# First layer's down-projection: context's product in scaled fp16 parts with four weight blocks in flight, and each late conditioning sum behind an operand's remainder

## The chip, the cores and the metric

One Trainium2 chip, one of its cores. A core has a matrix engine (TensorE: PE in the profile, with PEld for its weight loads), a vector engine (VectorE, DVE), a scalar engine (ScalarE, ACT), GpSimd (POOL) and SyncE (SP); each runs its own list of instructions in order and waits on semaphores for the others. Transfers are issued by queues: SP's carries the loads here, POOL's the stores and a few loads. The metric is the device time of one execution in microseconds, the median of several runs.

## The reference, cut to what matters

Two layers of a diffusion backbone over 1024 latent tokens and 256 context tokens of width 1024. Each layer ends with a gated feed-forward block, whose down-projection `(silu(u @ w_gate) * (u @ w_up)) @ w_down` has an inner width of 2816 (22 blocks of 128). It acts on the latent tokens in both layers and on the context tokens in the first. The residual sum is gated by a conditioning vector: six vectors per layer come from `silu(c) @ ada_w + ada_b`, and six more from the context's own vector with the same weights.

```python
h_lat = h_lat + g2 * swiglu(modulate(rms_norm(h_lat, norm2_g[i]), sh2, sc2),
                            ffn_w_gate[i], ffn_w_up[i], ffn_w_down[i])
if not last:
    h_ctx = h_ctx + cg2 * swiglu(modulate(rms_norm(h_ctx, norm2_g[i]), csh2, csc2),
                                 ffn_w_gate[i], ffn_w_up[i], ffn_w_down[i])
```

All is in fp32, to an accuracy that one pass of a short type doesn't give. The kernel therefore writes an operand as a high part in a shorter type and a remainder, and makes three matmuls for one: high by high, high by remainder, remainder by high.

## The kernel before, in words

The feed-forward of a layer is `ffn`. Its eleven iterations (`i`, two of the 22 blocks each) make the gated hidden values of the latent tokens in a seven-product scheme (Winograd's form of Strassen's), store them as operands of the down-projection, and make the sums of weight quarters that this scheme needs (`sums`: four loads of `down`, vector sums, stores). On the way `bound` takes largest absolute values of what goes into the down-projection, an ACT pass with an accumulator each (L1956); a reduction on DVE and one over the partitions on POOL turn them into scales (`ds`), which bring the operands into fp16's range. Context's hidden values are made before the iterations and stored to `hidc`, 256 KB for two blocks.

`down` follows. Its first part is seven products, p0 to p6. Each is eleven steps, and a step has two operands of 512 columns. `operands` loads both (two loads of 256 KB on SP), ACT makes the high parts in fp16 (L2248, one instruction for each operand) and DVE the remainders (L2249, likewise); twelve matmuls of 128x512 follow (L2258), four groups of columns by three. The last step of a product has its parts in fp32r, not fp16. Two sets of accumulators take turns, and a product's results leave by four DVE instructions at its end (`evict`, L2280).

In the first layer, the late conditioning sums run in between. `ada_stream` has 56 blocks of conditioning weights. The first 30 are done in `ffn`; of the last 26, one is taken at every second step of p0 to p4, and two in p5 (`next(todo)`). Such a block is a load of 512 KB by POOL into one of three tiles of its own and two sums on DVE, each over two instructions of 128x512 and accumulator readings (`step`, whose passes are L571).

After p6, in the first layer alone, comes context's product: 22 weight blocks (`kb`, the loop that ends at L2384). For each, the hidden values are loaded by POOL (128x256) and a weight block of 512 KB by SP, into one of four `ws` tiles or, for every fifth block (`kb % 5 == 4`: 4, 9, 14 and 19), into a tile of the pool S4. ACT casts the high part to fp32r (L352), DVE takes the remainder (L354), and 24 matmuls of 128x256 follow (L2381), eight groups by three. The parts of the weights lie in `pair1()`: one tile tag for the high parts and one for the remainders, two tiles deep. So two blocks are in flight. Beside this product run the normalizations of the results for the next layer (`norm_block`, L673 to L676), which `hook()` strings in.

What sets the order: a scheduler orders every engine's list from the order in the program and its own estimates of time. `with self.follow(x):` has what is inside issued after instruction x. In `ada_stream` only the load of a late block stands in such a bracket (behind the last load by POOL), its sums do not.

Of the kernel before, what the change touches and what calls it, by code (L numbers as in the profile page):

```python
# [10 lines left out]
F32 = mybir.dt.float32  # L11
F32R = mybir.dt.float32r
F16 = mybir.dt.float16
# [245 lines left out]
class Builder:  # L259
# [324 lines left out]
    def ada_stream(self, groups, n):  # L584

        blocks = [(l, m, m * 8 + k, conds) for l, m, conds in groups for k in range(8)]

        def step(b, st):
            l, m, nb, conds = b
            self.ada_block(l, nb, [st[:, :512], st[:, 512:]], conds)  # L590
            if nb % 8 == 7:
                self.ada_done(l, m, conds)

        own = [self.S4() for _ in range(3)]
        for k in range(0, n, 3):
            with self.follow(self.last_hi):
                for t, b in zip(own, blocks[k:k + 3]):
                    self.lda(t, self.a["ada_w"][b[0], b[2]])
            yield
            with self.follow(self.last_lo):  # L600
                for t, b in zip(own, blocks[k:k + 3]):
                    step(b, t)
            yield
        for k, b in enumerate(blocks[n:]):
            t = own[k % 3]
            with self.follow(self.last_ldr):
                self.ldr(t, self.a["ada_w"][b[0], b[2]])
            step(b, t)
            yield

    def late_groups(self, ms, where):
# [1457 lines left out]
    def ffn(self, l, u, h, hs, second, after, keep=None, begun={}):  # L2069
# [6 lines left out]
        nm = 4 * (n2 - 1)  # L2076
        def sums(i):

            w = a["down"][l]
            t = [self.S2() for _ in range(4)]  # L2080
            a21, a22, a11, a12 = t
            with self.follow(self.last_ld):
                for x, (k, r) in zip(t, ((0, 1), (1, 1), (0, 0), (1, 0))):
                    self.ld(x, w[2 * i + k, r])
            nc.vector.tensor_tensor(a22, a21, a22, ADD)  # L2085
            nc.vector.tensor_tensor(a21, a11, a21, SUB)
            nc.vector.tensor_tensor(a11, a22, a11, SUB)
            nc.vector.tensor_tensor(a12, a12, a11, SUB)
            for j, (k, x) in enumerate((("S1", a22), ("S2", a11), ("S3", a21), ("S4", a12))):
                self.ldr(sops[i][k], x)  # L2090
                if i < n2 - 1:
                    self.bound(x, mx[:, 4 * i + j:4 * i + j + 1])

        todo = iter(())
        if u is None:
            mx, ds = self.mx, self.ds
        else:
            self.ds = ds = self.C(6)
            wsums = self.C(4 * NFB)
            self.mx = mx = wsums[:, :2 * nm]  # L2100
        if l == 0:
            self.pad(self.pt, PAD_T)
        if u is not None:
# [40 lines left out]
        def bounds(i, ts):  # L2144

            for j, t in enumerate(ts):
                self.bound(t, mx[:, nm + 4 * i + j:nm + 4 * i + j + 1])
            if i == n2 - 2:
                nc.vector.tensor_reduce(ds[:, 4:6], mx.rearrange("p (k n) -> p k n", k=2), axis=AX, op=MAX)
                nc.gpsimd.partition_all_reduce(ds[:, 0:2], ds[:, 4:6], channels=P, reduce_op=bass.bass_isa.ReduceOp.max)  # L2150

        self.junk = self.S2(mybir.dt.bfloat16)
        prev = None
        for i in range(NFB // 2):
            g, up = begun.get((i, 0)), begun.get((i, 1))
            if g is None or not g.whole:
                wg = self.wino_pair(l, i, 0, g and g.w)
                with self.follow(self.last_x if l and i == 1 else None):
                    w = next(wg)
                    next(wg)  # L2160
            if g is None:
                g = Steps(self.wino_steps(w, lambda: self.either(self.G)))
                g.to(1)
            if prev is not None:
                prev[0].to(7)
                ts = finish(i - 1, prev[1])
            wu = iter(())
            if up is None or not up.whole:
                wu = self.wino_pair(l, i, 1, up and up.w)
                w = next(wu)  # L2170
                if up is None:
                    up = Steps(self.wino_steps(w, lambda: self.either(self.TK)))
            if i == 0:
                for k, _ in enumerate(second):
                    if k == 11:
                        next(wu, None)
            with self.follow(self.last_x if l and i == 1 else None):
# [12 lines left out]
            g.to(7)  # L2190
            add = self.last_add
            gate = dict(self.res)
            inv = self.wsc[(l, 0)][1] if l in self.half else 1.0
            for k in ((0, 0), (1, 1), (0, 1)):
                nc.scalar.activation(gate[k], gate[k], AF.Silu, scale=inv)
            t = self.G()
            nc.scalar.activation(t, gate[(1, 0)], AF.Silu, scale=inv)
            gate[(1, 0)] = t
            next(ahead, None)
            up.to(5)  # L2200
            next(ahead, None)
            if i == n2 - 1:
                with self.follow(add):
                    nc.vector.tensor_scalar(ds[:, 0:2], ds[:, 0:2], 1e-30, 1.0 / 8192.0, op0=MAX, op1=MUL)
                nc.vector.reciprocal(ds[:, 2:4], ds[:, 0:2])
            prev = (up, gate)
            for k in (2 * i - 6, 2 * i - 5) if l == 1 else (9, 10) if i == 9 else (i,) if i < 9 else ():
                if 0 <= k < n2:
                    sums(k)
            if i == 0 and u is not None:  # L2210
                with self.follow(self.last_hi):
                    for t in self.cond:
                        for x in t:
                            nc.scalar.activation(x, x, AF.Silu)
                next(todo, None)
            if i < 10:
                next(todo, None)
# [2 lines left out]
        prev[0].to(7)  # L2220
        finish(n2 - 1, prev[1])
        ad = self.ada[(l, 0)][:, 40:48]
        nc.vector.tensor_scalar(ad, ad, ds[:, 0:1], ds[:, 1:2], op0=MUL, op1=MUL)
        if l == 0:
            nc.vector.tensor_scalar(ad, ad, self.wsc[(0, 1)][1], None, op0=MUL)
        self.down(l, bops, sops, hidc, hs, h, todo, after, keep, ds)

    def down(self, l, bops, sops, hidc, hs, h, todo, after, keep, ds):  # L2230
# [5 lines left out]
        def operands(asrc, bsrc, own, last):  # L2236
            if last:
                hi, lo = self.S4(F32R), self.S4(F32R)
            else:
                t = self.S4(F16, 2048)  # L2240
                hi, lo = t[:, :1024], t[:, 1024:]
            f = self.S4() if own < 2 else self.W("ws", "ws")
            self.ld(f[:, :512], asrc)
            self.ld(f[:, 512:], bsrc)
            for c in (0, 512):
                s = ds[:, 2 + c // 512:3 + c // 512]
                x, y = hi[:, c:c + 512], lo[:, c:c + 512]
                self.last_hi = nc.scalar.activation(x, f[:, c:c + 512], AF.Copy, scale=s).ins  # L2248
                self.last_lo = nc.vector.scalar_tensor_tensor(y, f[:, c:c + 512], s, self.raw_part(x), op0=MUL,  # L2249
                                                              op1=SUB).ins  # L2250
            return hi, lo
# [105 lines left out]
        if l == 0:  # L2357
            done = (x for g in (done, after(1)) for x in g)
            acc = [self.PP() for _ in range(4)]
            for kb in range(NFB):  # L2360
                if kb and kb % 2 == 0:
                    hook()
                if kb in (4, 8, 12, 16):
                    load_h((kb // 2 - 2, kb // 2 - 1), 2)
                t = self.S2(F32R)
                f = t[:, 256:].bitcast(F32)
                with self.follow(self.last_ldr):
                    self.ldr(f, hidc[kb // 2][:, kb % 2])
# [699 lines left out]
```

## Time and profile before

| | us |
|---|---|
| median of 3 runs | 2881.32 (2877.79 to 2889.66) |
| profiled execution | 2878.91 |
| its span | 2877.1 |
| PE busy in the span | 2729.7 (95%) |
| DVE busy | 2125.5 (74%) |
| ACT busy | 1582.5 (55%) |
| POOL busy | 509.5 (18%) |

PE is busy for nearly all of the span, so a gap in PE's work is what a change can win, along with time in which PE works at a lower clock. Of the span, 960 to 1300 us is most of the first layer's eleven iterations of `ffn`; `down` follows, p0 up to about 1342, p1 to p6 up to 1546 us, and context's product up to 1627 us, where the second layer begins. The prediction shows the rows of these stretches. A row of a timeline has start, duration, engine, line, operation, result and operands, and in brackets how long the engine had been idle and what ended that. A row of a group has busy time, mean nanoseconds of one instruction and, behind the second bar, the idle time ahead of such instructions.

### The profile page before, as it was taken

How to read it: one execution, taken by the hardware profiler on the slowest of the kernel's cores; microseconds unless marked ns; L12 is line 12 of the kernel's file. 1: busy time of each engine (PE TensorE's matmuls, PEld its weight loads, DVE VectorE, ACT ScalarE, POOL GpSimd, SP SyncE). 2: the span in 40 equal slices, each digit the busy share in tenths (PEclk: the TensorE clock that was granted, in tenths of full speed). 3: DMA queues.
4: the chain of work that ended last, by engine and by line, in shares of the span. 5: the costliest groups of instructions: out<-in, count | busy, mean ns of one | idle time of the engine just before them, and what ended most of it. 6: DMA issues, size and time to landing. Idle time of an engine off the chain costs nothing. (4 is left out here: it accounts for less than half of the span.)

```text
span 2877.1 us, 44401 instructions
## 1 busy us (share of the span) xinstructions
PE 2729.7 (95%) x15570; PEld 1853.1 (64%) x15570; DVE 2125.5 (74%) x3845; ACT 1582.5 (55%) x2919; POOL 509.5 (18%) x817
## 2 busy tenths in 40 slices
PE   6999888999999999998899999999999999999998
PEld 3877677788897444443346888888887544444444
DVE  5678788768777989976875636777786877776775
ACT  3534235443587666664464425777775555564663
POOL 2110223351000111121200001323222011221000
PEclk9999999999999999999999999999999999999999
DMA  7355636656556777779983435878875235664873
GB/s 261 101 164 164 190 117 191 224 190 228 211 185 214 253 259 270 274 274 336 318 273 112 139 117 150 198 176 188 201 242 198 103 121 202 219 212 176 283 227 108
DMA packets 307277, 580.45 MB, mean 202 GB/s; under 512 B 82792, under 2 KB 129578, under 8 KB 307054
## 3 DMA queue, kind: packets, MB, share of 16 engines
q1 hardware_dynamic: 239790, 375.73, 41.7%
q0 software_dynamic: 53760, 158.38, 16.0%
q10 hardware_dynamic: 13504, 43.52, 4.3%
q8 instruction: 122, 2.00, 0.3%
q14 instruction: 101, 0.83, 0.1%
HBM read 430.17 MB, written 119.80 MB: 191 GB/s over the span
## 5 line engine op out<-in xcount | busy, mean ns | idle before, releaser
L2023 PE MATMUL ps<-s,s 128*128 128x512 f16 x2280 | 510.5, 379 | 2.4 <-ACT g L2028 2.2
L2023 PEld LDWEIGHTS <-s 128*128 128x128 f16 x2640 | 258.2, 98 | 315.2 <-issue 3.7
L348 PE MATMUL ps<-s,wh 128*128 128x256 f32 (+1 forms) x1784 | 410.5, 333 | 9.6 <-ACT wh L352 5.8
L2258 PE MATMUL ps<-s 128*128 128x512 f16 (+2 forms) x1404 | 319.9, 378 | 24.6 <-DVE s L2249 24.2
L348 PEld LDWEIGHTS ps<-s,wh 128*128 128x128 f32 x1784 | 299.4, 191 | 45.0 <-ACT wh L352 7.9
L2258 PEld LDWEIGHTS <-s 128*128 128x128 f16 x1716 | 167.2, 99 | 226.6 <-issue 39.6
L348 PE MATMUL ps<-s,wl 128*128 128x256 f32 (+1 forms) x892 | 272.4, 332 | 4.1 <-DVE wl L354 4.1
L2248 ACT ACTIVATE s<-s,c 128x512 f16<-128x512 f32 (+1 forms) x300 | 199.2, 714 | 118.4 <-DMA s<-d 54.5
L348 PE MATMUL pq<-s,wh 128*128 128x512 f32 (+1 forms) x840 | 256.0, 385 | 0.2 <-DVE s L937 0.2
L348 PE MATMUL ps<-s,s 128*128 128x65 f16 (+4 forms) x2748 | 230.8, 235 | 17.7 <-DMA s<-tk 9.3
L2249 DVE SCALAR_TENSOR_TENSOR s<-s,c,s 128x512 f16<-128x512 f32 (+1 forms) x300 | 206.8, 746 | 25.6 <-ACT s L2248 25.6
L339 POOL DMA_DIRECT2D d<-s x245 | 133.1, 544 | 509.3 <-DVE s L2085 92.5
L2023 PE MATMUL ps<-s,hl 128*128 128x512 f16 x924 | 213.6, 379 | 1.3 <-ACT hl L1876 1.3
L354 DVE TENSOR_TENSOR wl<-ws,wh 128x1024 fp32r<-128x1024 f32 (+1 forms) x102 | 121.3, 1191 | 106.4 <-ACT wh L352 102.0
L352 ACT CAST wh<-ws 128x1024 fp32r<-128x1024 f32 (+1 forms) x102 | 103.3, 1016 | 156.9 <-PE ps L348 89.8
L2023 PEld LDWEIGHTS <-hl 128*128 128x128 f16 x1056 | 103.2, 98 | 126.0 <-ACT hl L1876 1.5
L348 PEld LDWEIGHTS ps<-s,wl 128*128 128x128 f32 x892 | 167.2, 191 | 23.2 <-DVE wl L354 5.9
L348 PEld LDWEIGHTS pq<-s,wh 128*128 128x128 f32 x840 | 150.0, 189 | 22.7 <-DVE s L937 0.6
L348 PE MATMUL pq<-s,wl 128*128 128x512 f32 (+1 forms) x420 | 159.0, 379 | 0.0
L348 PEld LDWEIGHTS ps<-s,s 128*128 128x128 f32 (+1 forms) x828 | 130.9, 194 | 26.2 <-PE ps L348 2.7
L1877 DVE SCALAR_TENSOR_TENSOR s<-t,c,s 128x512 f16<-128x512 f32 x176 | 128.2, 746 | 18.6 <-ACT s L1876 18.6
L1876 ACT ACTIVATE s<-t,c 128x512 f16<-128x512 f32 x176 | 118.6, 713 | 6.5 <-DVE t L2002 4.5
(535 smaller groups left out, 5271.0 us busy)
## 6 DMA issues: line engine op xcount, KB each, us to landing
s<-d SPq DMA_DIRECT2D x315, 256.0 KB, 5.1
d<-s POOLq DMA_DIRECT2D x229, 256.0 KB, 3.8
s<-in_down SPq DMA_DIRECT2D x150, 256.0 KB, 6.1
ws<-in_gate SPq DMA_DIRECT2D x42, 512.0 KB, 4.0
ws<-in_up SPq DMA_DIRECT2D x42, 512.0 KB, 4.5
s<-in_ada_w POOLq DMA_DIRECT2D x34, 512.0 KB, 6.6
d<-s SPq DMA_DIRECT2D x60, 256.0 KB, 2.6
s<-in_ada_w ACTq DMA_DIRECT2D x30, 512.0 KB, 7.7
```

Source lines behind the costliest of these rows:

```text
L339: self.last_ldr = self.nc.gpsimd.dma_start(out, in_).ins
L348: self.last_mm = self.nc.tensor.matmul(o, l, r, start=st, stop=sp).ins
L352: self.last_hi = nc.scalar.copy(hi, src).ins
L354: self.last_lo = eng.tensor_tensor(lo, src, hi.bitcast(F32), SUB).ins
L1876: self.last_hi = self.nc.scalar.activation(hi, src, AF.Copy, scale=s).ins
L1877: self.last_lo = self.nc.vector.scalar_tensor_tensor(lo, src, s, hi, op0=MUL, op1=SUB).ins
L2023: nc.tensor.matmul(ps, x[:, sl], y, start=first and j == 0 and x is wh and y is xh, stop=j == 3 and x is wl, skip_group_check=True)
L2248: self.last_hi = nc.scalar.activation(x, f[:, c:c + 512], AF.Copy, scale=s).ins
L2249: self.last_lo = nc.vector.scalar_tensor_tensor(y, f[:, c:c + 512], s, self.raw_part(x), op0=MUL, op1=SUB).ins
L2258: m = nc.tensor.matmul(acc[j][:, c0:c1], x[:, sl], y[:, xs], start=first and k == 0, stop=last and k == 2, skip_group_check=True)
```

## The change

Three things are edited, all for the first layer's feed-forward.

First, `step(b, t)` of a late conditioning block is put into `with self.follow(self.last_lo)`: its sums are issued after the latest operand's remainder.

Second, context's product takes its operands in fp16: the hidden values with one scale, the weights with the scale that the latent product's weights have (`split_scaled`, L1876 and L1877 before: ACT makes the scaled high part, DVE the remainder). The parts of a block now lie in one tile of `hl()`, 2048 wide in fp16, high part and remainder side by side. `hl()` takes the two tags of `pair1()` in turn, two tiles each, so four blocks can be in flight.

Third, for the scale of the hidden values: `ffn` of the first layer loads each of the eleven pieces of `hidc` once more (SP, 256 KB) and takes a bound of each (ACT). The bounds of the last sums, which were left out before, are now taken too (four more in each layer). The reductions of all bounds become two or three for the three groups and one over the partitions, and context's gate is multiplied by the inverse scales.

```diff
@@ ada_stream
             with self.follow(self.last_ldr):
                 self.ldr(t, self.a["ada_w"][b[0], b[2]])
-            step(b, t)
+            with self.follow(self.last_lo):
+                step(b, t)
             yield
@@ ffn: sums(i)
                 self.ldr(sops[i][k], x)
-                if i < n2 - 1:
-                    self.bound(x, mx[:, 4 * i + j:4 * i + j + 1])
+                self.bound(x, mx[:, 4 * i + j:4 * i + j + 1])
...
+        hm, raw, inv, dsc = (self.cw[:, c:c + w] for c, w in ((0, n2), (n2, nd), (n2 + 3, nd), (n2 + 6, nd)))
@@ ffn: bounds(i, ts)
+            for k, x in hidden:
+                self.bound(x, hm[:, k:k + 1])
+            hidden.clear()
             if i == n2 - 2:
-                nc.vector.tensor_reduce(ds[:, 4:6], mx.rearrange("p (k n) -> p k n", k=2), axis=AX, op=MAX)
-                nc.gpsimd.partition_all_reduce(ds[:, 0:2], ds[:, 4:6], channels=P, reduce_op=bass.bass_isa.ReduceOp.max)
+                for k, x in enumerate((mx[:, :4 * n2], mx[:, 4 * n2:], hm)[:nd]):
+                    nc.vector.tensor_reduce(raw[:, k:k + 1], x, axis=AX, op=MAX)
+                nc.gpsimd.partition_all_reduce(inv, raw, channels=P, reduce_op=bass.bass_isa.ReduceOp.max)
@@ ffn: behind sums(k) of an iteration
+                if l == 0:
+                    x = self.S2()
+                    with self.follow(self.last_ld):
+                        self.ld(x.rearrange("p (n k) -> p n k", n=2), hidc[k])
+                    hidden.append((k, x))
@@ ffn: end
+            ad = self.ada[(0, 1)][:, 40:48]
+            nc.vector.tensor_scalar(ad, ad, inv[:, 0:1], inv[:, 2:3], op0=MUL, op1=MUL)
@@ down: context's product
-                t = self.S2(F32R)
-                f = t[:, 256:].bitcast(F32)
+                t = self.S2(F16, 1024)
+                f = t[:, 512:].bitcast(F32)
                 with self.follow(self.last_ldr):
                     self.ldr(f, hidc[kb // 2][:, kb % 2])
                 with self.follow(self.last_hi), self.follow(self.last_lo):
-                    self.split(f, t[:, :256], t[:, 256:])
+                    self.split_scaled(f, t, ds[:, 2:3])
                 f = self.W("ws", "ws") if kb % 5 < 4 else self.S4()
-                wh, wl = self.pair1()
                 with self.follow(mark[0]), self.follow(mark[1]), self.follow(mark[2]):
                     self.ld(f.rearrange("p (r k) -> p r k", r=2), w[kb].rearrange("r p k -> p r k"))
-                    self.split(f, wh, wl)
+                    wh, wl = self.split_scaled(f, self.hl(), ds[:, 0:1])
```

The functions that it calls: `split_scaled` is a copy with a scale on ACT into `t[:, :w]` and a multiply and subtract on DVE into `t[:, w:2 * w]`; `hl()` returns a tile of tag "wh" or "wl" in turn.

The scheduler moves instructions with it. The first place is DVE's list at the start of p1. L571's four rows are one sum over two passes; `ps` with L2280 (L2293 in the changed kernel) are p0's results leaving, and L2249 (L2262) with "x2" are the two remainders of one step. Before:

```order
L2280 SCALAR_TENSOR_TENSOR s_2951_12901<-ps_12758,c_97,s_2951_12901 128x512
L571 ISA s_2411_9427,ah_13161<-s_2411_9427,s_2362_9154,c_101 128x512
L571 ISA ah_13161 128x1
L571 ISA s_2411_9427,c_99<-s_2411_9427,s_2362_9154,ah_13161 128x512
L571 ISA c_99 128x1
L2249 SCALAR_TENSOR_TENSOR s_2974_13068<-s_2975_13069,c_7523,s_2974_13068 128x512 x2
L571 ISA s_2412_9428,ah_13213<-s_2412_9428,s_2362_9154,c_101 128x512
L571 ISA ah_13213 128x1
L571 ISA s_2412_9428,c_99<-s_2412_9428,s_2362_9154,ah_13213 128x512
L571 ISA c_99 128x1
L571 ISA s_2410_9426,ah_13257<-s_2410_9426,s_2362_9154,c_101 128x512
```

Now:

```order
L2293 SCALAR_TENSOR_TENSOR s_2960_12940<-ps_12797,c_97,s_2960_12940 128x512
L571 ISA s_2411_9429,ah_13104<-s_2411_9429,s_2360_9153,c_101 128x512
L571 ISA ah_13104 128x1
L571 ISA s_2411_9429,c_99<-s_2411_9429,s_2360_9153,ah_13104 128x512
L571 ISA c_99 128x1
L2262 SCALAR_TENSOR_TENSOR s_2983_13107<-s_2984_13108,c_317,s_2983_13107 128x512 x2
L2262 SCALAR_TENSOR_TENSOR s_2985_13127<-s_2986_13128,c_317,s_2985_13127 128x512 x2
L571 ISA s_2409_9427,ah_13148<-s_2409_9427,s_2360_9153,c_101 128x512
L571 ISA ah_13148 128x1
L571 ISA s_2409_9427,c_99<-s_2409_9427,s_2360_9153,ah_13148 128x512
L571 ISA c_99 128x1
L2262 SCALAR_TENSOR_TENSOR s_2992_13159<-s_2993_13160,c_317,s_2992_13159 128x512 x2
```

Where one or two sums stood between a step's remainders and the next step's, one sum now stands behind two steps' remainders, and so on to the end of p4.

The second place is DVE's list in the middle of context's product of the changed kernel: `hl_15096` is weight block 13, `hl_15172` block 15, `hl_15251` block 17, `hl_15139` block 14 (whose weights are in a tile of S4), and the 128x256 rows are hidden values.

```order
L1878 SCALAR_TENSOR_TENSOR hl_15096<-ws_15094,c_317,hl_15096 128x1024
L1878 SCALAR_TENSOR_TENSOR s_3238_15133<-s_3238_15133,c_317 128x256
L647 RECIPROCAL st_14977<-st_14977 128x4
L1878 SCALAR_TENSOR_TENSOR hl_15172<-ws_15170,c_317,hl_15172 128x1024
...
L677 SCALAR_TENSOR_TENSOR s_3245_15200<-t_15205,c_99,s_3245_15200 128x512
L1878 SCALAR_TENSOR_TENSOR hl_15251<-ws_15249,c_317,hl_15251 128x1024
L674 SCALAR_TENSOR_TENSOR t_15280<-s_2999_13223,c_99,t_15046 128x512
L674 SCALAR_TENSOR_TENSOR t_15284<-s_3000_13225,c_99,t_15046 128x512
L1878 SCALAR_TENSOR_TENSOR s_3259_15288<-s_3259_15288,c_317 128x256
L1878 SCALAR_TENSOR_TENSOR hl_15139<-s_3239_15137,c_317,hl_15139 128x1024
L1878 SCALAR_TENSOR_TENSOR s_3241_15166<-s_3241_15166,c_317 128x256
```

Before, the blocks stood in their order 13, 14, 15, 16, 17; now blocks 15 and 17 stand ahead of block 14, on ACT's list too.

The third place is SP's list in an iteration of `ffn`. Before:

```order
L333 DMA s_2835_12064<-in_down 128x512
L333 DMA s_2836_12065<-in_down 128x512
L333 DMA ws_12425<-in_gate 128x1024
L333 DMA ws_12508<-in_up 128x1024
L333 DMA ws_12510<-in_up 128x1024
```

Now:

```order
L333 DMA s_2841_12087<-in_down 128x512
L333 DMA s_2842_12088<-in_down 128x512
L333 DMA s_2843_12105<-d_7520 128x512
L333 DMA ws_12459<-in_gate 128x1024
L333 DMA ws_12542<-in_up 128x1024
```

The load of context's hidden values (`d_7520`) stands between the four loads for `sums` and the second gate load of the next iteration; the rest is as before.

More of the change, by code (lines that the diff above doesn't have):

```diff
@@ L2075, in ffn @@
         hidc = [self.DR([P, 2, 256]) for _ in range(n2 if u is not None else 0)]
-        nm = 4 * (n2 - 1)
         def sums(i):
@@ L2090, in sums @@
                 self.ldr(sops[i][k], x)
-                if i < n2 - 1:
-                    self.bound(x, mx[:, 4 * i + j:4 * i + j + 1])
+                self.bound(x, mx[:, 4 * i + j:4 * i + j + 1])
         todo = iter(())
+        nd = 2 if u is None else 3
+        hm, raw, inv, dsc = (self.cw[:, c:c + w] for c, w in ((0, n2), (n2, nd), (n2 + 3, nd), (n2 + 6, nd)))
         if u is None:
-            mx, ds = self.mx, self.ds
+            mx = self.mx
         else:
-            self.ds = ds = self.C(6)
             wsums = self.C(4 * NFB)
-            self.mx = mx = wsums[:, :2 * nm]
+            self.mx = mx = wsums[:, :8 * n2 - 4]
         if l == 0:
@@ L2146, in bounds @@
             for j, t in enumerate(ts):
-                self.bound(t, mx[:, nm + 4 * i + j:nm + 4 * i + j + 1])
+                c = 4 * (n2 + i) + j
+                self.bound(t, mx[:, c:c + 1])
+            for k, x in hidden:
+                self.bound(x, hm[:, k:k + 1])
+            hidden.clear()
             if i == n2 - 2:
-                nc.vector.tensor_reduce(ds[:, 4:6], mx.rearrange("p (k n) -> p k n", k=2), axis=AX, op=MAX)
-                nc.gpsimd.partition_all_reduce(ds[:, 0:2], ds[:, 4:6], channels=P, reduce_op=bass.bass_isa.ReduceOp.max)
+                for k, x in enumerate((mx[:, :4 * n2], mx[:, 4 * n2:], hm)[:nd]):
+                    nc.vector.tensor_reduce(raw[:, k:k + 1], x, axis=AX, op=MAX)
+                nc.gpsimd.partition_all_reduce(inv, raw, channels=P, reduce_op=bass.bass_isa.ReduceOp.max)
         self.junk = self.S2(mybir.dt.bfloat16)
+        hidden = []
         prev = None
@@ L2192, in ffn @@
             gate = dict(self.res)
-            inv = self.wsc[(l, 0)][1] if l in self.half else 1.0
+            ginv = self.wsc[(l, 0)][1] if l in self.half else 1.0
             for k in ((0, 0), (1, 1), (0, 1)):
-                nc.scalar.activation(gate[k], gate[k], AF.Silu, scale=inv)
+                nc.scalar.activation(gate[k], gate[k], AF.Silu, scale=ginv)
             t = self.G()
-            nc.scalar.activation(t, gate[(1, 0)], AF.Silu, scale=inv)
+            nc.scalar.activation(t, gate[(1, 0)], AF.Silu, scale=ginv)
             gate[(1, 0)] = t
@@ L2203, in ffn @@
                 with self.follow(add):
-                    nc.vector.tensor_scalar(ds[:, 0:2], ds[:, 0:2], 1e-30, 1.0 / 8192.0, op0=MAX, op1=MUL)
-                nc.vector.reciprocal(ds[:, 2:4], ds[:, 0:2])
+                    nc.vector.tensor_scalar(inv, inv, 1e-30, 1.0 / 8192.0, op0=MAX, op1=MUL)
+                nc.vector.reciprocal(dsc, inv)
             prev = (up, gate)
@@ L2222, in ffn @@
         ad = self.ada[(l, 0)][:, 40:48]
-        nc.vector.tensor_scalar(ad, ad, ds[:, 0:1], ds[:, 1:2], op0=MUL, op1=MUL)
+        nc.vector.tensor_scalar(ad, ad, inv[:, 0:1], inv[:, 1:2], op0=MUL, op1=MUL)
         if l == 0:
             nc.vector.tensor_scalar(ad, ad, self.wsc[(0, 1)][1], None, op0=MUL)
-        self.down(l, bops, sops, hidc, hs, h, todo, after, keep, ds)
+            ad = self.ada[(0, 1)][:, 40:48]
+            nc.vector.tensor_scalar(ad, ad, inv[:, 0:1], inv[:, 2:3], op0=MUL, op1=MUL)
+        self.down(l, bops, sops, hidc, hs, h, todo, after, keep, dsc)
     def down(self, l, bops, sops, hidc, hs, h, todo, after, keep, ds):
@@ L2245, in operands @@
             for c in (0, 512):
-                s = ds[:, 2 + c // 512:3 + c // 512]
+                s = ds[:, c // 512:c // 512 + 1]
                 x, y = hi[:, c:c + 512], lo[:, c:c + 512]
```

## The prediction

> **What bounds the kernel now.** I read the table of busy time by stretch first, to find where PE, busy for 95% of the span, is not. Its columns: stretch, length, then busy time and count of PE, PEld, DVE, ACT and POOL, PE's granted clock, the DMA share, GB/s.
>
> ```profile
> core 0: us, PE busy (x) PEld busy (x) DVE busy (x) ACT busy (x) POOL busy (x), PEclk, DMA share, GB/s
> 960.00:1300.00 340.00, 337.81 (x1566) 153.12 (x1565) 292.36 (x540) 221.10 (x433) 59.56 (x110) 1.00 0.77 271
> 1300.00:1341.90 41.90, 41.73 (x193) 19.71 (x192) 27.78 (x52) 20.45 (x33) 7.00 (x13) 1.00 0.82 295
> 1341.90:1408.00 66.10, 41.80 (x162) 17.82 (x161) 57.32 (x127) 18.00 (x28) 21.27 (x41) 0.92 0.93 327
> 1408.00:1546.00 138.00, 138.00 (x638) 67.58 (x637) 95.71 (x145) 82.06 (x127) 2.55 (x5) 1.00 0.70 242
> 1546.00:1627.20 81.20, 68.97 (x540) 66.76 (x539) 52.62 (x75) 40.13 (x63) 2.93 (x7) 0.92 0.46 144
> 1627.20:1700.00 72.80, 72.80 (x325) 60.25 (x324) 33.91 (x69) 24.96 (x40) 0.37 (x1) 1.00 0.38 121
> ```
>
> Before 1341.9 and from 1408 to 1546 PE sets the pace, without a gap. It falls short in two stretches: p1 (1341.9 to 1408, 24.3 us idle) and context's product (1546 to 1627.2, 12.2 us idle), both also at clock 0.92. After 1627.2 PE is full again, so what comes earlier there is not lost behind it.
>
> In p1 the groups of PE say who ends its waits, and the late sums (L571) by stretch say when they run:
>
> ```profile
> L2258 PE MATMUL ps<-s 128*128 128x512 f16 x91 | 25.9, 407 | 24.3 <-DVE s L2249 24.2
> 1326.00:1341.90 15.90, 6.08 (x16) 1.00 1.04 401
> 1341.90:1408.00 66.10, 33.27 (x88) 0.92 0.93 327
> 1408.00:1546.00 138.00, 0.00 (x0) 1.00 0.70 242
> ```
>
> Nearly all of the idle time ends with a remainder from DVE. A sum is four instructions, so 22 of the 26 late sums fall into p1 (33.27 us, 1.51 us each), the first four ahead of it, and none into the 138 us behind. Is DVE late itself, or its operands? The timelines of PE, ACT and DVE:
>
> ```profile
> 1345.17 1.02 PE L2258 MATMUL ps<-s 128*128 128x512 f16 x4 [3.14 <-DVE s L2249]
> 1336.21 1.33 ACT L2248 ACTIVATE s<-s,c 128x512 f16<-128x512 f32 x2 [4.68 <-DMA s<-in_down]
> 1350.94 2.72 DVE L2280 SCALAR_TENSOR_TENSOR s<-ps,c,s 128x512 f32<-128x512 f32 x4
> 1355.04 1.41 DVE L2249 SCALAR_TENSOR_TENSOR s<-s,c,s 128x512 f16<-128x512 f32 x2
> 1356.37 0.74 DVE L571 CUSTOM_DVE_ANT_0 s<-s,s,c 128x512 f32<-128x512 f32 x1
> ...
> 1359.30 1.41 DVE L2249 SCALAR_TENSOR_TENSOR s<-s,c,s 128x512 f16<-128x512 f32 x2
> ```
>
> The high parts made at 1336.21 are those of the operands whose remainders start at 1355.04: loads and ACT are some 18 us ahead, DVE is not. Between the remainders of two steps stand two sums (1356.4 to 1359.3). So in p1 the sums on DVE hold PE, and the transfers don't, though their share is 0.93.
>
> **Part one, the sums behind remainders.** A matmul of 128x512 takes 138.00/638 = 0.2163 us where PE is full, so p1's 162 need 35.0 us; they take 66.1. The loss is 31.1 us: 24.3 idle and 6.8 at the lower clock. With one sum behind two steps' remainders, DVE needs 2 x 1.41 + 1.51 = 4.33 us for what takes PE 24 x 0.2163 = 5.19. Over a product of eleven steps: 11 x 1.41 + 5.5 x 1.51 + 2.72 for the results = 26.5 us against PE's 28.6. DVE now fits, at 93%, with the sums spread to the end of p4.
>
> What stays: the gap of 3.1 us at 1345.17, since the sums ahead of it stand where they stood. At p1's third step: after the second step's remainders come the four results, a sum and the next remainders, so that 1.41 + 2.72 + 1.51 + 1.41 = 7.05 us on DVE meet 5.19 on PE: 1.9. I add 1.5 for the starts of p2 to p5, where DVE has to make up the same 2.72 (estimated; bounds 0, and 9.6 as worked out under the rivals). Gain 31.1 - 3.1 - 1.9 - 1.5 = 24.6, bounds 15 and 26. The transfers allow it: the same 22 loads of 0.5 MB, which run beside p1 at 327 GB/s, are spread over p1 to p4, and the row above shows 401 GB/s carried.
>
> **Part two, context's product.** Who ends its waits (groups), and how a gap looks on PE and ACT:
>
> ```profile
> L2381 PE MATMUL ps<-s,wh 128*128 128x256 f32 x352 | 66.0, 291 | 9.5 <-ACT wh L352 9.5
> L2381 PEld LDWEIGHTS ps<-s,wh 128*128 128x128 f32 x351 | 56.7, 200 | 10.8 <-ACT wh L352 10.3 <-issue 0.5
> L2381 PE MATMUL ps<-s,wl 128*128 128x256 f32 x176 | 51.5, 292 | 2.7 <-DVE wl L354 2.7
> 1556.79 0.39 PE L2381 MATMUL ps<-s,wh 128*128 128x256 f32 x2
> 1557.13 0.39 PE L2381 MATMUL ps<-s,wh 128*128 128x256 f32 x2
> 1561.09 0.51 PE L2381 MATMUL ps<-s,wh 128*128 128x256 f32 x2 [3.11 <-ACT wh L352]
> 1562.72 0.63 PE L2381 MATMUL ps<-s,wh 128*128 128x256 f32 x2
> 1565.29 0.61 PE L2381 MATMUL ps<-s,wh 128*128 128x256 f32 x2
> 1559.99 1.04 ACT L352 CAST wh<-s 128x1024 fp32r<-128x1024 f32 x1 [4.07 <-DMA s<-in_down]
> ```
>
> The gap of 3.1 us is the load of a block in S4, which ACT waited for 4.07 us. Three matmuls take 1557.13 - 1556.79 = 0.34 us, 0.113 each, so 528 need 59.8 us. The 81.2 us are these, 12.2 idle, about 1.5 for the other 12 matmuls (estimated at 0.12 each), and so some 7.7 for slow matmuls behind gaps: from 1562.72 to 1565.29 four times three take 0.64 each. A gap of this kind costs about 1.7 us on top of itself (five or six triples with 0.3 each).
>
> Does fp16 make the matmuls cheaper? The last product of the second layer has fp16 matmuls of this shape:
>
> ```profile
> 2855.10 1.28 PE L2258 MATMUL ps<-s 128*128 128x256 f16 x10
> 2856.21 0.40 PE L2258 MATMUL ps<-s,s 128*128 128x256 f32 x2
> L2258 PEld LDWEIGHTS <-s 128*128 128x128 f16 x1716 | 167.2, 99 | 226.6 <-issue 39.6
> L1877 DVE SCALAR_TENSOR_TENSOR hl<-ws,c,hl 128x1024 f16<-128x1024 f32 x39 | 49.9, 1281 | 15.5 <-ACT hl L1876 15.4
> L1876 ACT ACTIVATE hl<-ws,c 128x1024 f16<-128x1024 f32 x39 | 44.6, 1144 | 39.4 <-DMA ws<-in_gate 19.5 <-DMA ws<-in_up 17.3 <-DVE c L1869 2.6
> 1553.75 1.41 DVE L673 SCALAR_TENSOR_TENSOR t<-s,c,t 128x512 f32<-128x512 f32 x2
> L354 DVE TENSOR_TENSOR s<-s 128x256 fp32r<-128x256 f32 x19 | 7.9, 418 | 0.0
> ```
>
> Ten in 1.11 us are 0.111 each, 1.2 us less over all 528: I take no gain. The weight loads fall from 200 to 99 ns, but lie beside the matmuls, which are not faster for it. The Trainium skill (TensorE: Matmul & The Clock Gate, "Weight-path perf modes" and "Back-to-back issue gap") says that weights that aren't fp32 load about twice as fast, and that both operations together set a matmul's spacing. The trace agrees with the halving, not with a spacing that follows it here.
>
> Four blocks in flight hold 4 x 24 x 0.113 = 10.9 us of PE's work ahead, where two held 5.4. The first four blocks can be split before p6's operands, and the `ws` loads follow as tiles come free, so the gaps at blocks 4, 9 and 19 and the short ones should close. One gap is made by the order: blocks 15 and 17 stand ahead of block 14 on ACT and DVE, and 17 can be split only when PE has done 13, whose tile it takes. PE then wants 14, and waits for 17's high part (1.14), its remainder (1.28), two normalizations (1.41), a small split (0.42) and 14's remainder (1.28), with a little for the small split on ACT: 5.7 us, and 1.7 for slow matmuls behind it. So the product takes 59.8 + 1.5 + 5.7 + 1.7 = 68.7 us, a gain of 12.5; bounds 6 (the gap at 9 us, and two of the old ones of 3.1 left) and 20 (no gap).
>
> **Part three, what is added in `ffn`.** Eleven loads on SP, fifteen bounds on ACT, four reductions and small steps on DVE (under 1 us, beside DVE's 47 us of idle in the 340 and behind nothing that PE awaits).
>
> ```profile
> L1956 ACT ACTIVATE s<-s 128x512 bf16<-128x512 f32 x46 | 28.5, 620 | 5.6 <-DVE s L2137 5.5
> L1956 ACT ACTIVATION_READ_ACCUMULATOR s<-s 128x1 f32 x46 | 8.7, 189 | 0.0
> 1116.72 0.33 SPq L333 DMA_DIRECT2D ws<-in_gate  x1
> 1117.14 1.83 SPq L333 DMA_DIRECT2D s<-in_down  x4
> 1128.93 0.33 SPq L333 DMA_DIRECT2D ws<-in_gate  x1
> ```
>
> A bound is 0.81 us, so 15 are 12.1, against 119 us in which ACT idles in the 340. The last iteration gets six of them, 4.9 us, just before PE needs ACT to empty accumulators, which is where the cover is thinnest: if all of it showed, 4.9. The layer's four other extra bounds, in the second, are hidden alike. A load takes SP 1.83/4 = 0.46 us to issue, and the queue idles from 1118.97 to 1128.93 there, 10 us an iteration, waiting for a weight tile. Its operand was stored long before. I take 1 us for this part, bounds 0 and 5.
>
> **Sum**, against the profiled execution's 2878.9: - 24.6 - 12.5 + 1 = 2842.8. The median of the runs shown stands 2.4 above that execution, so the forecast is 2845.
>
> **The rivals.**
> *DVE becomes the bound in p1 to p4.* At 93% it has 2 us of slack in a product, and each product begins with the results ahead of a sum and a step's remainders. If the 1.9 us come at each start of p2 to p5, with 0.5 for the clock (6.8/24.3 of a gap), that is 9.6, and the gain is 31.1 - 3.1 - 1.9 - 9.6 = 16.5: 2853. For it: DVE is 57.3 of 66.1 us busy now. Against it: ACT and loads are 18 us ahead, so DVE may run ahead in the middle of a product.
> *Context's product gains little:* S4's loads, which wait for a tile of p6, still come late, and the gap at block 14 comes on top; then part two brings some 4 us, and the time is 2854.
> *The weight loads set the pace* (the rule above): 528 x (0.113 - 0.099) = 7.4 us more, 2838. The row of 0.111 speaks against it. With it goes the case that block 14's gap does not appear, 2838 too.
> *The change does not do what it says:* the sums run late, the remainders wait for p1's sums elsewhere, or both half-gains meet new waits: above 2867, within 0.5% of before.
> *Slower: the SP queue is held.* Its loads are in order. If the added load waits for its tile, whose last user is a store, beyond the 10 us of idle time, the gate weights behind it come late, and PE with them, in each of eleven iterations. The two gains, 36 us, are gone at 3.3 us beyond the cover each; at 5 it is 2881 - 36 + 55 = 2900. Against it: 10 us is long beside a store.
>
> **How the numbers follow.** Forecast 0.58; DVE bound 0.13; little from context's product 0.10; faster weights or no gap 0.05; no difference 0.09; slower 0.05. A measurement of this kernel can tell 0.5%, 14.4 us, from no change, so the first four are faster: 0.86. The range takes in the first four with the bounds: low 2881.3 - 26 - 20 + 0 = 2835, taken as 2833 for the runs' spread; high, 15 and 6 gained and 5 lost with it, 2865.
>
> **What would show it.** The late sums spread from 1326 to about 1460, one for two steps; PE's idle time behind L2262 in p1 under 7 us, and none of note in p2 to p4; p1 at a clock near 1.0. In context's product one gap of about 6 us, at block 14, that ends with ACT or DVE, weight loads near 99 ns and triples of 0.34 us; `ffn` as long as before, within 2 us. It is wrong if PE waits for remainders in p2 to p4 for 10 us or more, if the product stays above 75 us, or if the iterations of `ffn` grow.

## The result and the profile after

| | before | changed |
|---|---|---|
| median of 5 runs, us | 2881.32 (2877.79 to 2889.66) | 2855.75 (2846.16 to 2859.92) |
| profiled execution, us | 2878.91 | 2851.5 |
| its span, us | 2877.1 | 2849.7 |

The ratio is 0.9902, 95% interval 0.9877 to 0.9927: faster by 1%, 25.6 us by the medians. The forecast was 2845, in a range of 2833 to 2865.

To see where it went, I took the starts of the first matmul of each stage from PE's timeline. "ffn" runs from the first gate or up matmul of the first layer to p0's first; "product" is context's, up to the end of its last matmul, and the second layer's `ffn` too begins at its first gate or up matmul. The rows below are durations in us.

| stage | before | changed | difference |
|---|---|---|---|
| start to ffn | 910.4 | 912.8 | +2.4 |
| ffn, first layer | 396.7 | 407.1 | +10.4 |
| p0 to p6 | 238.9 | 214.0 | -24.9 |
| context's product | 81.3 | 67.5 | -13.7 |
| to the second layer's ffn | 632.0 | 629.6 | -2.4 |
| ffn, second layer | 397.6 | 398.6 | +1.0 |
| its down, to the end of matmuls | 208.8 | 208.8 | 0 |

Both gains are there at nearly their forecast size, and 10 us of them are lost in `ffn`, where the forecast had 1. The first and the fifth stage are not touched by the change. In the twelve profiles of this study they range from 908.8 to 920.2 and from 624.3 to 640.2, while the second layer's down is 208.8 us in all. So a time can differ by several us with nothing that was edited, and what an edit does is read from its stage.

Busy time by stretch of the changed kernel (columns as in the prediction's first table): p0, p1, p2, p3, p4, p5.

```profile
core 0: us, PE busy (x) PEld busy (x) DVE busy (x) ACT busy (x) POOL busy (x), PEclk, DMA share, GB/s
1319.90:1353.70 33.80, 33.78 (x156) 16.22 (x155) 24.54 (x44) 16.32 (x26) 6.99 (x13) 1.00 0.84 298
1353.70:1388.80 35.10, 31.54 (x133) 14.57 (x132) 30.84 (x60) 16.12 (x24) 3.69 (x7) 0.90 0.99 365
1388.80:1417.50 28.70, 28.70 (x133) 13.90 (x132) 25.88 (x50) 21.24 (x33) 2.64 (x5) 1.00 1.00 362
1417.50:1446.20 28.70, 28.70 (x134) 13.97 (x134) 26.27 (x53) 15.22 (x24) 3.18 (x6) 1.00 0.91 316
1446.20:1474.80 28.60, 28.60 (x133) 13.90 (x132) 25.96 (x50) 13.08 (x20) 12.75 (x24) 1.00 0.90 306
1474.80:1503.50 28.70, 28.70 (x134) 13.92 (x134) 24.12 (x35) 19.44 (x30) 0.00 (x0) 1.00 0.95 337
```

PE is full from p2 on, with DVE at 26 of 28.7 us, but the transfers are nearly full as well, 0.90 to 1.00. The late sums now run to the end of p4, as the count of L571 by the same stretches shows:

```profile
1353.70:1388.80 35.10, 10.36 (x28) 0.90 0.99 365
1388.80:1417.50 28.70, 7.57 (x20) 1.00 1.00 362
1417.50:1446.20 28.70, 9.06 (x24) 1.00 0.91 316
1446.20:1474.80 28.60, 7.54 (x20) 1.00 0.90 306
1474.80:1503.50 28.70, 0.00 (x0) 1.00 0.95 337
```

PE's timeline from p0 to the end of context's product has three rows with a wait of over 0.2 us, the last two at weight block 14; the group row of the product's matmuls agrees with them:

```profile
1358.34 1.86 PE L2271 MATMUL ps<-s 128*128 128x512 f16 x4 [3.56 <-DVE s L2262]
1575.84 0.61 PE L2393 MATMUL ps<-s,hl 128*128 128x256 f16 x2 [3.43 <-ACT hl L1877]
1578.73 22.67 PE L2393 MATMUL ps<-s,hl 128*128 128x256 f16 x190 [2.28 <-DVE hl L1878]
L2393 PE MATMUL ps<-s,hl 128*128 128x256 f16 x528 | 60.5, 278 | 5.7 <-ACT hl L1877 3.4 <-DVE hl L1878 2.3
```

In `ffn` most of the waits are new. The gate and up matmuls on PE, first before, then changed (groups of 910 to 1342 and of 912 to 1345 us):

```profile
L2023 PE MATMUL ps<-s,s 128*128 128x512 f16 x1320 | 294.4, 379 | 2.4 <-ACT g L2028 2.2 <-ACT s L1876 0.2
```

```profile
L2024 PE MATMUL ps<-s,s 128*128 128x512 f16 x1320 | 295.1, 380 | 10.3 <-ACT g L2029 10.2 <-ACT s L1877 0.2
```

L2029 is the copy that empties an accumulator on ACT. The largest of these waits, on PE and on ACT:

```profile
1118.31 4.34 PE L2024 MATMUL ps<-s,s 128*128 128x512 f16 x12 [2.95 <-ACT g L2029]
1108.20 1.15 ACT L1877 ACTIVATE hl<-ws,c 128x1024 f16<-128x1024 f32 x1 [3.51 <-DMA ws<-in_up]
1108.27 0.84 ACTq L336 DMA_DIRECT2D s<-in_gate  x2
1116.06 1.06 ACT L1846 ACTIVATE s<-s 128x1024 f32<-128x1024 f32 x1 [4.87 <-DMA s<-in_gate]
1117.67 0.59 ACT L2029 COPY g<-ps 128x512 f32<-128x512 f32 x1 [0.46 <-ACT s L1846]
```

L1846 (L1845 before) is a pass over the second layer's weights (`scan`), which are loaded on ACT's own queue. It waits for its load until 1116.06, and the copy that PE needs stands behind it. The load was issued late because its place on ACT is behind a split that waited for `ws<-in_up`. In the kernel before, the copy stood ahead of that pass in the same iteration:

```profile
1102.62 0.59 ACT L2028 COPY g<-ps 128x512 f32<-128x512 f32 x1 [1.08 <-PE ps L2023]
1107.65 1.06 ACT L1845 ACTIVATE s<-s 128x1024 f32<-128x1024 f32 x1 [4.45 <-DMA s<-in_gate]
```

ACT waits nearly as long there, but nobody waits for ACT. ACT's lists show it as a change of order, before and changed:

```
before:
L1956 ACTIVATE s_2364_9160,c_7524<-s_2571_10408 128x512
L2028 COPY g_10612<-ps_10479 128x512
L1845 ACTIVATE s_2393_9237,c_9236<-s_2393_9237 128x1024
L336 DMA s_2393_9237<-in_gate 128x1024
L1845 ACTIVATE s_2394_9238,c_9236<-s_2394_9238 128x1024
changed:
L1957 ACTIVATE s_2362_9159,c_7523<-s_2572_10416 128x512
L1846 ACTIVATE s_2391_9236,c_9235<-s_2391_9236 128x1024
L336 DMA s_2391_9236<-in_gate 128x1024
L2029 COPY g_10623<-ps_10489 128x512
L1846 ACTIVATE s_2392_9237,c_9235<-s_2392_9237 128x1024
```

### The profile page after: what moved, and what is told of

Read it like the earlier page. It is cut to its first block, busy times and chain, and to the rows that moved or that the text cites. A ratio compares the mean times of both kernels' runs of the same rounds, so it can differ in the third digit from the quotient of the medians.

```text
span 2849.7 us, 44445 instructions
## 1 busy us (share of the span) xinstructions
PE 2717.6 (95%) x15570; PEld 1836.6 (64%) x15570; DVE 2127.8 (75%) x3849; ACT 1597.2 (56%) x2957; POOL 510.0 (18%) x817
## 5 line engine op out<-in xcount | busy, mean ns | idle before, releaser
L2262 DVE SCALAR_TENSOR_TENSOR s<-s,c,s 128x512 f16<-128x512 f32 (+1 forms) x300 | 209.3, 748 | 31.7 <-ACT s L2261 31.6
L348 PEld LDWEIGHTS ps<-s,wl 128*128 128x128 f32 x892 | 167.5, 191 | 24.6 <-DVE wl L354 7.8
L354 DVE TENSOR_TENSOR wl<-ws,wh 128x1024 fp32r<-128x1024 f32 (+1 forms) x84 | 99.4, 1186 | 93.0 <-ACT wh L352 88.7
L352 ACT CAST wh<-ws 128x1024 fp32r<-128x1024 f32 (+1 forms) x84 | 84.5, 1009 | 134.7 <-PE ps L348 82.0
L1877 ACT ACTIVATE s<-t,c 128x512 f16<-128x512 f32 x176 | 118.0, 714 | 5.6 <-DVE t L2003 4.5
```

The lines of the kernel that those rows point to most:

```text
L348: self.last_mm = self.nc.tensor.matmul(o, l, r, start=st, stop=sp).ins
L352: self.last_hi = nc.scalar.copy(hi, src).ins
L354: self.last_lo = eng.tensor_tensor(lo, src, hi.bitcast(F32), SUB).ins
L1877: self.last_hi = self.nc.scalar.activation(hi, src, AF.Copy, scale=s).ins
```

## The experiments

**What made ffn longer.** Theory: the added bounds changed the order of ACT's list, and the order costs the time. Rival: the added work itself costs it (12 us of ACT, or SP's loads in front of the weights).

The sums alone, on the kernel before:

```diff
-            step(b, t)
+            with self.follow(self.last_lo):
+                step(b, t)
```

> The kernel before with the bracket around the late sums alone (each behind an operand's remainder). If part one's reading holds (DVE with the sums in front held PE), p0 to p6 take about 214 us as in the changed kernel, where they took 238.9, and ffn stays at 396.7 us from its first gate matmul to p0's first: the time is 25 us below before, about 2856. Rival: the gain needs the other parts too, or is paid back where the late sums now lie (p2 to p5): 2866 or more.

Measured: 2854.0 (ratio 0.9904, interval 0.9880 to 0.9929); p0 to p6 212.6 us, `ffn` 398.5. So part one stands on its own and brings what it brings in the changed kernel, and `ffn` is within 2 us of before. As the product is 79.7 us here, this one edit is as fast as the whole change: the rest of the change won 13.7 us and lost 10.4.

Part three alone, on the kernel before:

```diff
+                self.bound(x, mx[:, 4 * i + j:4 * i + j + 1])
...
+            for k, x in hidden:
+                self.bound(x, hm[:, k:k + 1])
...
+                    with self.follow(self.last_ld):
+                        self.ld(x.rearrange("p (n k) -> p n k", n=2), hidc[k])
```

> The kernel before with part three alone: the eleven loads on SP, the fifteen bounds and the wider reductions in ffn; sums and context's product as before (the scale of the hidden values is computed and not used). Theory: these bounds change ACT's list, so that an accumulator copy stands behind a pass over the next layer's weights that waits for its load; ffn takes about 407 us for 396.7 and the time is about 10 above before, 2891. Rival: the lost 10 us of ffn were a chance of that execution or come from the other two parts; then ffn stays within 2 us of 396.7 and the time is 2881.

Measured: 2897.1 (1.0051, 1.0033 to 1.0070), slower by 16 us; `ffn` 408.7 us, 12.0 more than before, and PE's waits for the copies 10.0 us as in the changed kernel. What the time grew beyond that lies mainly in the stage up to the second layer's `ffn` (640.2 us for 632.0), which no edit touches. So part three makes `ffn` longer, by 12.0 us here and 10.4 in the changed kernel. Over all twelve profiles `ffn` takes 404.0 to 408.7 us in the five whose ACT list there is the changed kernel's, and 395.8 to 399.9 in the other seven. This run does not yet say by what.

Then the order alone, all loads and bounds kept:

```diff
-            nc.scalar.copy(t, ps)
+            self.last_snap = nc.scalar.copy(t, ps).ins
...
-            with self.follow(self.last_hi):
+            with self.follow(self.last_hi), self.follow(self.last_snap):
                 if k > 1:
                     nc.scalar.activation(t, t, AF.Abs, accum_out=sums[:, k - 2:k - 1])
```

> The changed kernel with one addition: the passes over the next layer's weights are issued behind the latest accumulator copy. All loads and bounds stay. Theory (the order of ACT's list costs it, not the work that was added): ffn back to 397 to 399 us, PE's waits for L2029's copies from 10.2 to about 2 us, the time 9 below the changed kernel's 2855.8, about 2847. Rival (ACT's added 12 us, or SP's added loads in front of the weights, cost it): ffn stays at 405 or more and the time at 2856.

Measured: 2842.8 (0.9874, 0.9850 to 0.9899); `ffn` 395.8 us. With the copies ahead of the passes, PE's waits for them are gone (groups on PE from 908 to 1304.5 us):

```profile
L2025 PE MATMUL ps<-s,s 128*128 128x512 f16 x1296 | 289.3, 379 | 1.1 <-ACT s L2030 0.6 <-ACT g L2030 0.3 <-ACT s L1878 0.2
```

The rival falls: the added work is all there and costs nothing. The order of ACT's list is shown to be the cause. The bracket moved the passes behind both copies of an iteration and some issues of their loads ahead of the split, so it is the order as a whole; the copy's place and the late loads were not told apart.

The other way to the same end, without the eleven loads and bounds:

```diff
+                nc.vector.tensor_reduce(hm[:, fb:fb + 1], t[:, :256], axis=AX, op=MAX, apply_absolute_value=True)
                 self.ldr(hidc[fb // 2][:, fb % 2], t[:, :256])
...
-                    with self.follow(self.last_ld):
-                        self.ld(x.rearrange("p (n k) -> p n k", n=2), hidc[k])
-                    hidden.append((k, x))
```

> The changed kernel without the eleven loads and eleven of the bounds in ffn: the largest absolute value of context's hidden values is taken on DVE where they are made (22 reductions of 128x256), before the iterations. ACT's list in the iterations is then that of before. Theory: ffn at 397 us, the 22 reductions hidden beside PE ahead of it, the time about 2846. Rival: DVE's 22 reductions hold PE where the hidden values are made, by up to 22 x 0.4 = 9 us, which gives back what ffn wins: 2855.

Measured: 2839.4 (0.9858, 0.9835 to 0.9882); `ffn` 396.2 us and the stage ahead of it 910.3, as long as before. The 22 reductions take DVE 9.2 us there and delay nothing.

**What makes context's product shorter.** Theory: the lookahead of four blocks. Rival: fp16 itself.

```diff
-                    wh, wl = self.split_scaled(f, self.hl(), ds[:, 0:1])
+                    wh, wl = self.split_scaled(f, self.W("wh", "hl", F16, 2048), ds[:, 0:1])
```

> The changed kernel with the parts of context's weight blocks in one tag of two tiles, so two blocks in flight, still in scaled fp16 (and then in their order on ACT and DVE, 14 ahead of 15 and 17). Part two's reading (the gain is the lookahead, fp16 matmuls are no cheaper): the gaps at the S4 blocks 4, 9, 14 and 19 come back, and the product takes 75 to 81 us where it takes 67.5. Rival (the faster fp16 weight loads or the smaller operands made the gain): 62 to 68 us.

Measured: the product takes 84.7 us, the time of the one run is 2882.1. The gaps stand where they stood, at blocks in S4, two of them on ACT:

```profile
1555.12 1.15 ACT L1877 ACTIVATE hl<-s,c 128x1024 f16<-128x1024 f32 x1 [4.40 <-DMA s<-in_down]
1595.78 1.15 ACT L1877 ACTIVATE hl<-s,c 128x1024 f16<-128x1024 f32 x1 [5.47 <-DMA s<-in_down]
```

That is 17 us more than with four in flight and 3.5 more than fp32r with two. fp16 wins nothing by itself; it halves what a block occupies, and that makes room for the lookahead. All gaps of the kernel before lie at blocks in S4, though, so keeping all blocks in `ws` might have closed them with two in flight as well; that was not tried.

The gap at block 14 was predicted from the order of the lists. Its test, all blocks in `ws`, which leaves blocks 13 to 17 in their order:

```diff
-                f = self.W("ws", "ws") if kb % 5 < 4 else self.S4()
+                f = self.W("ws", "ws")
```

> The changed kernel with all 22 weight blocks of context's product in the four ws tiles, none in S4; blocks 13 to 17 then stand in their order on ACT and DVE. Theory (the one gap of 5.7 us at block 14 is made by the order of the lists): no gap, product 60.5 to 62 us. Rival (the fifth tile was needed, since a block of 512 KB takes longer to load than PE needs for it): gaps of 1 to 3 us at several blocks, product 67 or more.

Measured: the product takes 59.5 us without a gap; one run at 2835.9. (`ffn` was 404.0 here, 3 less than in the changed kernel; its order is that kernel's.) 59.48/528 = 0.1127 us is what a matmul costs, as the 0.113 of fp32r before. The fifth tile did harm and was not needed. But this run took away the late load of block 14 together with the order. In the changed kernel PE had run out of work at 1572.4, and of block 14 ACT and DVE show:

```profile
1574.64 1.15 ACT L1877 ACTIVATE hl<-s,c 128x1024 f16<-128x1024 f32 x1 [0.53 <-DMA s<-in_down]
1575.67 1.41 DVE L674 SCALAR_TENSOR_TENSOR t<-s,c,t 128x512 f32<-128x512 f32 x2
1577.39 1.28 DVE L1878 SCALAR_TENSOR_TENSOR hl<-s,c,hl 128x1024 f16<-128x1024 f32 x1
```

DVE's list set the end of the gap, as predicted: two normalizations and a small split stand ahead of the remainder. The high part, however, waited last for the block's own weights, whose load SP issued only at 1569.31, behind one into a `ws` tile. So with 14 ahead of 17 on ACT and DVE alone, the first 3.4 us of the gap would have stayed; the order and the late load were not told apart.

**What held PE in p1 before.** The prediction said DVE's work, and not the transfers. Two tests, the first on the changed kernel with the sums closer together:

```diff
-                if p < 5 and i % 2 or p == 5 and i < 2:
+                if p < 3:
```

> The changed kernel with a late sum taken at every step of p0 to p2, not at every second one of p0 to p4; each still stands behind an operand's remainder. If DVE's capacity is what counts (1.41 + 1.51 = 2.92 us a step against PE's 2.60, and 2.72 for the results), PE falls behind in p1 and p2 and p0 to p6 take 222 to 232 us for 214. Rival (only that remainders no longer queue behind two sums in a row counts): 214 to 217.

Measured (one run, 2875.0): p0 to p6 take 235.1 us, beyond both: the bracket is kept and nearly the whole gain is gone, since p1 takes 53.8 us. A wait stands out among DVE's groups in p1 (1351.1 to 1404.9 us):

```profile
L571 DVE CUSTOM_DVE_ANT_0 s<-s,s,c 128x512 f32<-128x512 f32 x19 | 14.2, 748 | 9.8 <-DMA s<-in_ada_w 9.8
```

DVE itself waits for the sums' weights. The same wait is in the kernel before, in p1 (1341.9 to 1408 us):

```profile
L571 DVE CUSTOM_DVE_ANT_0 s<-s,s,c 128x512 f32<-128x512 f32 x22 | 16.5, 748 | 8.1 <-DMA s<-in_ada_w 8.1
```

So I took half of DVE's work on the sums away from the kernel before, and none of their loads. (A late block carries one sum of two passes, not two sums as the words on the kernel before have it: L571 has 104 rows, four for each of the 26 blocks.) The kernel leaves out the second pass:

```diff
-            step(b, t)
+            l, m, nb, conds = b
+            for c in conds:
+                self.nc.vector.tensor_tensor_reduce(t[:, :512], t[:, :512], self.cond[c][0], 1.0,
+                                                    self.adab[:, l * 48 + nb:l * 48 + nb + 1], MUL, ADD,
+                                                    self.ada[(l, c)][:, nb:nb + 1])
```

> The kernel before with half of each late conditioning sum left out (one DVE pass and reading for two); all 26 loads of 512 KB stay, as do their places ahead of remainders. In p1 of the kernel before DVE was busy 57.3 us and waited 8.1 for these loads. If DVE's work was what held PE, the 22 sums of p1 shrink by 0.75 each, 16.5 us, and p1 falls from 55.8 to about 40 us. Rival: the loads, each of which starts when the sum in its tile is done and lands some 6 us later, set the pace by themselves, and DVE waits where it worked: p1 stays above 50.

Measured (one run, 2878.1): p1 takes 56.3 us, as before (55.8; the stretch that the prediction calls p1, 1341.9 to 1408, is p1 and the first 11 us of p2). PE's p1 and DVE's waits in it (the stretch, then DVE's waits: total, times, longest):

```profile
1344.40:1400.70 56.30, 35.76 (x134) 15.14 (x134) 34.86 (x74) 15.62 (x22) 16.67 (x32) 0.88 0.99 369
```

```profile
DVE s L610 <- DMA s<-in_ada_w: 21.8, 14, 3.9
```

and p1 of the kernel before, cut at the same first and last matmuls:

```profile
1341.00:1396.80 55.80, 34.98 (x134) 15.02 (x133) 46.99 (x110) 13.89 (x20) 11.11 (x22) 0.91 0.94 339
```

DVE's work fell from 47.0 to 34.9 us and p1 by nothing; DVE waits instead, with the transfers at 0.99. The loads of the sums were enough to hold PE, through DVE's list: a remainder that is ready stands behind a sum whose weights have not come. Whether DVE's 47 us would also have held it, with the loads out of the way, was not tried; they are 18 more than the 28.7 us that PE needs. Nor do these runs say what limits the loads. Each is issued by POOL when the sum in one of three tiles is done (in p1 of the kernel before POOL waited 46.9 us for DVE there) and lands some 6 us later, so it may be the three tiles or the rate of the transfers; a fourth tile was not tried.

**Both repairs together, and what is left.** The early bound with all blocks in `ws`:

```diff
+                nc.vector.tensor_reduce(hm[:, fb:fb + 1], t[:, :256], axis=AX, op=MAX, apply_absolute_value=True)
...
-                f = self.W("ws", "ws") if kb % 5 < 4 else self.S4()
+                f = self.W("ws", "ws")
```

> The changed kernel with the hidden values' bound taken on DVE where they are made and all weight blocks of context's product in ws. If both readings hold, ffn 396.5 us and the product about 61.5: 16 us below the changed kernel, 2839 to 2841. Rival (one of the two gaps reappears elsewhere): 2845 or more.

Measured: 2830.9 median of five runs (2825.9 to 2832.2; ratio to before 0.9816, 0.9792 to 0.9840): `ffn` 395.8, p0 to p6 213.9, product 59.5. This beats both kernels, and is 9 us faster than expected, of which 2 are the product; the rest lies within what the stages that no edit touches vary by. What is left is p1, 35.0 us:

```profile
1345.65 1.87 PE L2267 MATMUL ps<-s 128*128 128x512 f16 x4 [3.21 <-DVE s L2258]
```

The last run moves the sums out of p0:

```diff
-                if p < 5 and i % 2 or p == 5 and i < 2:
+                if 0 < p < 6 and i % 2 or p == 6 and i == 1:
```

> The kernel with the early bound and all blocks in ws, and with the late sums at every second step of p1 to p5 and one in p6, none in p0. What is left of the gaps in p0 to p6 is one wait at p1's third step (3.6 us and slow matmuls behind it; p1 35.0 for 28.7), after p0's sums waited 8.8 us for their loads on DVE. If those sums make it, p1 takes 28.7 to 30 us, and the time is 5 to 6 below the kernel without this edit, 2825. Rival: p0's results and the first sum at p1's start make it (7.05 us of DVE against 5.19 of PE), wherever the sums begin: p1 stays near 35 and the time at 2831.

Measured: 2842.3 (0.9865, 0.9832 to 0.9899). p1 takes 28.7 us, so p0's sums did make that gap. (It lies in p1's first step, at its fifth matmul, and not in the third, as the expectation has it.) But p2 to p6 take 156.3 us for 145.0: a new wait of 5.9 us, now for ACT's high parts, with slow matmuls behind it, lies at the start of p6 (groups on PE from 1373 to 1530 us).

```profile
L2267 PE MATMUL ps<-s 128*128 128x512 f16 x480 | 114.3, 390 | 5.9 <-ACT s L2257 5.9
```

In p5, just ahead, the transfers are at a share of 0.99:

```profile
1459.00:1487.60 28.60, 28.60 (x133) 13.91 (x132) 25.83 (x46) 18.12 (x27) 12.80 (x24) 1.00 0.99 349
```

The sums' loads were there in the way of p6's operands; that it is they is argued from this share, not shown. The gap was moved and grew.

## Why the prediction was right or wrong

*Part one, size: right, in part by luck.* Forecast 24.6, measured 24.9 in the changed kernel, and 26.2 alone. DVE is busy 25.9 to 26.3 us in p2 to p4, for which 26.5 were worked out, and PE has no wait in them. Of the losses that should stay, 6.5 us in all, the gap at p1's start came where it was before, as 3.6 us for 3.1. The 1.9 us at p1's third step did not come (two of the experiments show 1.4 there), nor did the 1.5 us for the starts of p2 to p5. In their place came 2.8 us of slow matmuls behind the one gap, for which the sum has no term: p1 ran at a clock of 0.90, where "near 1.0" was forecast. The terms miss each way and add up to 6.4.

*Part one, reason: wrong in its second half.* "So in p1 the sums on DVE hold PE, and the transfers don't, though their share is 0.93." The operands' transfers were indeed 18 us ahead, but the sums' own loads were not, and half of DVE's work on the sums could go without any effect. The row that said so stood in the same view that I read PE's waits from, one engine further: L571's own idle time, 8.1 us in p1, ended by `in_ada_w`. The chain is PE behind a remainder, the remainder behind a sum, the sum behind its load. The forecast came out because spreading the sums thins their loads as much as their work; it would have come out by either reason, and so does not bear the one given out. The run with a sum at every step shows what the reading missed: by DVE's capacity it should have cost 8 to 18 us and cost 21.

*Part two: right.* 67.5 us for 68.7, the gap at block 14 5.7 us for 5.7, and as predicted first for ACT and then for DVE. The late load of block 14, which the prediction did not see, changed little, since DVE was later still. The 1.5 us for twelve other matmuls were not needed (the 59.5 us without a gap leave no room for them), and slow matmuls behind the gap cost 2.3 us for 1.7. Halved weight loads did not shorten the matmuls:

```profile
L2393 PEld LDWEIGHTS <-hl 128*128 128x128 f16 x528 | 52.3, 100 | 14.0 <-ACT hl L1877 3.7 <-DVE hl L1878 2.8 <-issue 0.8
```

A matmul takes 0.1127 us without gaps. The rule of the Trainium skill (TensorE: Matmul & The Clock Gate, "Back-to-back issue gap") that both operations set the spacing does not show at this shape.

*Part three: wrong, and it is the step that put the forecast 10 us low.* "I take 1 us for this part, bounds 0 and 5." It is 10.4 us in the first layer, and 1.0 in the second, whose `ffn` takes 398.5 or 398.6 us in every run with the four bounds added there and 397.6 in every run without. That the iterations of `ffn` grow is one of the prediction's own signs of being wrong. I had costed the added instructions against idle time of their engines, and in that they are free: with the copies ahead, all of them cost nothing. But the list in which they stand was laid out anew, and I compared the order of ACT's list in the product and not in `ffn`. What I named as thinnest cover, the last iteration, shows no such wait; the waits lie in six iterations before it, and only the first of them (1.9 us) was there before (2.2).

*Sum.* 10.75 us between forecast and median: 9.4 from part three, 1.9 because the median lies 4.3 above the profiled execution for 2.4, less 1.5 for the gains being larger, and 1.0 for the second layer.

*Rivals.* DVE as the bound did not come. With the sums closer PE waits for DVE again, but DVE then waits 9.8 us for weights, so that run is no proof of a bound by DVE's work. SP's queue was not what grew: its loads stayed in the kernel with the copies first, and `ffn` was as long as before.

## What to carry to other kernels

Idle time of an engine tells what added work costs only if the order of its list stays; where a scheduler lays the list out anew, look for an instruction that others wait for (a copy that frees an accumulator, an operand's remainder) which now stands behind one that waits for a transfer. When a row says that PE waits for DVE, read what DVE waits for at that place before calling DVE the bound, and test it by taking half of its work away. Work that comes in bunches with its own loads is better spread over the stretch in which the transfers have room than only put behind other work.

## What the runs showed of the hardware

Matmuls behind a gap of some three us are often slow, but not always. After 3.56 us in p1 of the changed kernel the next take 0.42 us each, for 0.2163 where PE is full:

```profile
1360.00 1.91 PE L2271 MATMUL pq<-s 128*128 128x512 f16 x4
1361.71 1.06 PE L2271 MATMUL ps<-s 128*128 128x512 f16 x2
```

and behind the 2.95 us at 1118.31 twelve matmuls last 4.34 us, where behind 1.53 us they last 2.75:

```profile
1040.83 2.75 PE L2024 MATMUL ps<-s,s 128*128 128x512 f16 x12 [1.53 <-ACT g L2029]
```

The length alone does not decide. Behind 2.34 us at 974.4 in the run with the sums alone the next take 0.42 us each, and behind 3.14 us in the kernel before four run at full speed:

```profile
1345.17 1.02 PE L2258 MATMUL ps<-s 128*128 128x512 f16 x4 [3.14 <-DVE s L2249]
```

The Trainium skill (TensorE: Matmul & The Clock Gate, "What's actually happening") has the clock halved after an idle window of about 3.4 us. The halving agrees, but 2.34 and 2.95 us were enough for it here. So a gap of some three us cost between once and twice its length here: p1 lost 6.4 us with 3.6 of idle time in the changed kernel, 6.3 with 3.2 in the one with both repairs, and 4.9 with two gaps of together 4.6 where all blocks were in `ws`.

The transfers reached 362 GB/s at a share of 1.00 with PE full (p2 of the changed kernel), so a share near one is no proof that PE is held: it was held at 339 GB/s and 0.94 in p1 before, and not at 362 in p2 after.
